# Latent attention's scores: three products of 96 rows become two passes of 128 rows and one of 32 rows on row groups

## The chip, the cores and the metric

One core of a Trainium2 chip runs the whole kernel. The metric is device time in microseconds (us): the time of one execution, median over the runs. Profiled executions come with a trace, whose span (from the first to the last instruction) is a little shorter than the execution's own time. PE is the matmul engine, PEld its loads of stationary operands, DVE the vector engine, ACT the scalar engine, POOL the third elementwise engine, and SP the queue that issues all DMAs of this kernel.

## The reference

One layer of an encoder trunk for 1024 tokens of 1024 channels in float32: a root-mean-square norm, one large input projection, then two attention mixers side by side (latent attention with 8 heads, and a dilated mixture), gated, projected, summed, projected again and added to the input. The change concerns the scores of latent attention. Cut to that:

```python
def mla_attention(c_q, c_kv, k_rope, positions, q_norm_g, kv_norm_g, w_uq, w_ukv):
    q = (rmsnorm(c_q, q_norm_g) @ w_uq).reshape(B, S, MLA_HEADS, MLA_QK_DIM)
    q = jnp.concatenate([q[..., :MLA_NOPE_DIM], rope(q[..., MLA_NOPE_DIM:], positions)], axis=-1)
    q = q * (MLA_QK_DIM ** -0.5)
    kv = (rmsnorm(c_kv, kv_norm_g) @ w_ukv).reshape(B, S, MLA_HEADS, MLA_NOPE_DIM + MLA_V_DIM)
    k_nope, v = kv[..., :MLA_NOPE_DIM], kv[..., MLA_NOPE_DIM:]
    k_pe = rope(k_rope[:, :, None, :], positions)
    k = jnp.concatenate([k_nope, jnp.broadcast_to(k_pe, (B, S, MLA_HEADS, MLA_ROPE_DIM))], axis=-1)
    ...
        s = jnp.einsum('bqhd,bkhd->bhqk', q_blk, k).astype(jnp.float32)
        p = jax.nn.softmax(s, axis=-1).astype(v.dtype)
        return jnp.einsum('bhqk,bkhd->bqhd', p, v)
```

A head's query and key have 96 channels: 64 of its own (`MLA_NOPE_DIM`) and 32 rotary ones (`MLA_ROPE_DIM`). The rotary part of the key is the same for all 8 heads.

## The kernel before

Every matmul of float32 values is done with operands in a rounded format (float32r in the code). A value is split into a high part, its rounding, and a low part, the rest. A product is then the sum of three matmuls, high by high, high by low and low by high, which `mm3` (lines 142 to 146) issues into one accumulator. In the profile these are the lines L144, L145 and L146, whatever the product is.

The kernel runs in stages. The first half (to about 530 us) does the projections. Inside it `latents` (line 338) makes the queries and keys of latent attention, half of the tokens at a time: `scaled` (line 390) scales a query tile of 128 channels by 512 tokens, splits it into the two halves of `mla_st` and stores them to HBM, the 64 own channels of each head to `s_qn`, the rotary ones to `s_qr`; the keys go to `s_kn` and the shared rotary key to `s_kp`. `mla_st` is a ring of two buffers. In this part a scheduler sets the order of instructions.

From about 538 us on the order is written out by hand. The dilated heads come first (to about 832 us), then latent attention (832 to about 1122 us), then the output projections. Latent attention is cut into 32 units; a unit is one head and 256 queries, that is two blocks b of 128 queries. `units` lists them: head by head, four units each, for heads 0 to 5; heads 6 and 7 alternate by two. `mla_tick(k, c)` (line 952) issues unit k in four steps c. Each step transposes a quarter of the unit's probabilities (`mla_transposes`, L852, four transposes into an accumulator called `bank`), splits them into a high part on ACT (L854) and a low part on DVE (L860), and multiplies an earlier quarter by the values (`mla_values`, L876 and L877). Step 0 also computes the scores of block 0 of the next unit, step 1 those of block 1; in steps 2 and 3 PE is given matmuls of other work (`feed`: the gates, then output projections). So in PE's queue the scores of unit k+1 stand among the transposes and value matmuls of unit k.

`mla_scores(k, b)` (line 814) is where the change is. A block's scores are 128 queries by 1024 keys and fill one of two accumulators, named `right` (block 0) and `left` (block 1) in the profile. For each half of the keys, 512 columns, it calls `mm3` with the 96 channels as rows: six matmuls per block, 12 per unit. Then DVE finds the maxima (L836) and ACT the exponentials (L844).

`mla_load_qk(h)` (line 799) loads a head's query and key from HBM to two buffers of 96 partitions that hold both parts, in five DMAs; it is called two heads ahead. `mla_load_v(h)` (line 809) loads its values into the ring `op_c`, of which it fills the first half of a place. All DMAs stand in one queue, SP, in the order of the code; one that must wait holds up those behind it. Buffers of the hand-ordered part appear as `at_r` and `at_f` in the profile.

At the end of the dilated part a last `combine` of dilated heads is spread over the first units of latent attention; it reads rows of factors from HBM (`s_rr`, twelve DMAs) and DVE multiplies by them (L1421).

Of the kernel before, what the change touches and what calls it, by code (L numbers as in the profile page):

```python
# [11 lines left out]
F32R = mybir.dt.float32r  # L12
# [7 lines left out]
S = 1024  # L20
# [40 lines left out]
class Net:  # L61
# [276 lines left out]
    def latents(self, up, lp, tp, pj):  # L338
# [4 lines left out]
        for half in range(2):  # L343
            c512 = slice(half * 512, half * 512 + 512)

            r = self.rcol[:, 4 * half:4 * half + 4]
# [7 lines left out]
            for t in range(4):  # L354
                c = self.lat[:, 4 * half + t]
# [15 lines left out]
            k = pt  # L371
# [18 lines left out]
            def scaled(src, dst):  # L390
                st = tp.tile([128, 2, 512], F32R, name="mla_st")
                nc.scalar.mul(st[:, 0], src, QK_SCALE)
                v.scalar_tensor_tensor(out=st[:, 1], in0=src, scalar=QK_SCALE, in1=st[:, 0].bitcast(F32), op0=ALU.mult, op1=ALU.subtract)
                self.dma(dst[:, :, c512], st)

# [3 lines left out]
            scaled(o1, self.qr[0])  # L399
            scaled(o2, self.qr[1])  # L400
            for j in range(4):
                scaled(up_q(slice(128 * j, 128 * j + 128)), self.qn[128 * j:128 * j + 128])
# [396 lines left out]
    def mla_load_qk(self, h):  # L799

        q, k = self.get("op_a", [96, 2, S], F32R), self.get("op_b", [96, 2, S], F32R)
        self.dma(q[0:64], self.qn[64 * h:64 * h + 64])
        for c in range(2):
            self.dma(q[64 + 16 * c:80 + 16 * c], self.qr[c][16 * h:16 * h + 16])
        self.dma(k[0:64], self.kn[64 * h:64 * h + 64])
        self.dma(k[64:96], self.kp)
        self.heads[h] = [q, k, None]

    def mla_load_v(self, h):

        vv = self.heads[h][2] = self.get("op_c", [128, 8, 128], F32R)
        self.dma(vv, self.mv.rearrange("(c p) x -> p c x", p=128)[:, :, 128 * h:128 * h + 128])

    def mla_scores(self, k, b):
# [7 lines left out]
        q, kk, _ = self.heads[h]  # L822
        qb = 2 * u + b
        qs = slice(128 * qb, 128 * qb + 128)
        s = self.get("s_mla", [128, S])
        for kb in range(2):
            ks = slice(512 * kb, 512 * kb + 512)
            self.mm3(s[:, ks], q[:, 0, qs], q[:, 1, qs], kk[:, 0, ks], kk[:, 1, ks], True, True)
        self.s[k, b] = s
# [693 lines left out]
    def run(self):  # L1523
        tc, nc = self.tc, self.nc
        with ExitStack() as ctx:
            dp = ctx.enter_context(tc.tile_pool(name="dram", bufs=1, space=DRAM))
            dt = lambda name, shape, d=F32: dp.tile(list(shape), d, name=name)
            self.qn, self.kn = dt("s_qn", (512, 2, S), F32R), dt("s_kn", (512, 2, S), F32R)
            self.qr, self.kp = dt("s_qr", (2, 128, 2, S), F32R), dt("s_kp", (32, 2, S), F32R)
# [163 lines left out]
```

## Time and profile before

| | us |
|---|---|
| median of 3 runs (lowest, highest) | 1263.55 (1259.07, 1266.88) |
| the profiled execution's own time | 1265.36 |
| its span | 1263.5 |
| PE busy, share of the span | 1214.5, 96% |
| DVE, ACT, POOL busy | 764.2, 621.0, 535.5 |
| mean granted PE clock | 0.992 |

Busy times are sums over the span; stages differ, so a share says little about one stage. A line of a timeline gives the start, the duration, the engine, the line of the kernel, the operation, what it writes and reads with partitions and elements, and, in brackets, the idle time of its engine just ahead and what ended it. Durations of matmuls overlap on PE: what one costs in a dense stream is the distance to the start of the next.

### The profile page before, as it was taken

What the parts mean: (1) busy time and instruction counts of PE and PEld (TensorE: products, weight loads), DVE (VectorE), ACT (ScalarE), POOL (GpSimd) and SP (SyncE); (2) the same over time, 40 slices, a digit from 0 to 9 for tenths busy, and PEclk for the clock granted to TensorE, in tenths of its full rate; (3) what the DMA queues carried; (4) which work ended last, traced back from release to release, by engine and by line L of the source; (5) the groups of instructions that cost most, each with busy time, mean ns of one, the idle gap of its engine ahead of it and who ended that gap; (6) DMA issues with size and microseconds to landing.
All of it is one profiled execution on the core that took longest, in us unless ns stands there. A gap on an engine that the chain in (4) does not pass through costs nothing.

```text
span 1263.5 us, 19551 instructions
## 1 busy us (share of the span) xinstructions
PE 1214.5 (96%) x6909; PEld 1063.2 (84%) x6909; DVE 764.2 (60%) x1373; ACT 621.0 (49%) x1300; POOL 535.5 (42%) x433
## 2 busy tenths in 40 slices
PE   8989999999999999999989899999899999989997
PEld 7979999788888888888878787978788888878886
DVE  7483524567567652345575776748777767659442
ACT  6533437344434345456554555636665655654232
POOL 2352217887777777445363230411420111157222
PEclk9989999999999999999999999999999999999999
DMA  9947675266556643497878797856543254234241
GB/s 325 274 152 264 224 283 159 84 177 167 138 135 158 169 125 117 129 260 205 207 207 211 186 259 191 240 156 165 154 140 105 81 126 125 93 101 167 84 150 50
DMA packets 131602, 212.99 MB, mean 169 GB/s; under 512 B 36841, under 2 KB 67121, under 8 KB 127601
## 3 DMA queue, kind: packets, MB, share of 16 engines
q1 hardware_dynamic: 131504, 211.75, 58.1%
q8 instruction: 54, 0.88, 0.3%
q14 instruction: 44, 0.35, 0.1%
HBM read 145.05 MB, written 66.65 MB: 168 GB/s over the span
## 4 chain that ended last, share of the span: by engine, by line
PE 72%; DMA 9%; DVE 8%; ACT 4%; issue 3%; POOL 2%; SPq 1%; ACTq 0%; DVEq 0%; POOLq 0%
PE bank L144 6%; PE bank L146 5%; PE bank L145 5%; PE bank L852 3%; PE st_a L144 2%; PE st_a L145 2%; PE st_a L146 2%; PE st_d L145 2%; PE st_c L145 2%; PE st_c L146 2%; PE st_d L146 2%; PE st_d L144 2%; PE st_c L144 2%; PE pj L144 2%; PE pj L145 2%
## 5 line engine op out<-in xcount | busy, mean ns | idle before, releaser
L151 POOL TENSOR_TENSOR w_l<-w_raw,w_h 128x512 fp32r<-128x512 f32 x188 | 246.7, 1326 | 300.1 <-ACT w_h L150 252.5
L150 ACT CAST w_h<-w_raw 128x512 fp32r<-128x512 f32 x188 | 112.4, 620 | 103.7 <-POOL w_raw L495 95.1
L144 PE MATMUL bank<-at_r,w_h 128*128 128x512 f32 x344 | 141.9, 412 | 5.6 <-DVE at_f L792 3.0
L860 DVE TENSOR_TENSOR at_r<-bank,at_r 128x512 fp32r<-128x512 f32 x128 | 87.9, 688 | 79.8 <-ACT at_r L854 79.5
L146 PE MATMUL bank<-at_r,w_l 128*128 128x512 f32 x344 | 135.3, 393 | 0.0
L145 PE MATMUL bank<-at_r,w_h 128*128 128x512 f32 x344 | 135.1, 393 | 0.0
L854 ACT CAST at_r<-bank 128x512 fp32r<-128x512 f32 x128 | 74.9, 585 | 81.0 <-PE bank L852 80.1
L144 PE MATMUL pj<-w_h,at_r 128*128 128x256 f32 x384 | 109.7, 286 | 0.0
L145 PE MATMUL pj<-w_l,at_r 128*128 128x256 f32 x384 | 109.4, 285 | 0.0
L146 PE MATMUL pj<-w_h,at_r 128*128 128x256 f32 x384 | 109.4, 285 | 0.0
L1116 ACT ACTIVATE at_f<-at_f,at_f 128x256 f32<-128x256 f32 x128 | 64.1, 501 | 70.8 <-DVE at_f L1109 70.7
L495 POOL TENSOR_TENSOR w_raw<-w_raw 128x512 f32<-128x512 f32 x64 | 83.7, 1308 | 0.0
L1135 DVE TENSOR_TENSOR at_r<-bank,at_r 128x512 fp32r<-128x512 f32 x64 | 44.0, 687 | 63.7 <-ACT at_r L1131 63.4
L852 PE MATMUL bank<-consts,at_f 128*128 128x128 f32 x512 | 77.0, 272 | 3.1 <-DVE at_r L860 2.0
L144 PEld LDWEIGHTS bank<-at_r,w_h 128*128 128x128 f32 x344 | 65.2, 190 | 16.8 <-DVE at_f L792 4.2
L146 PEld LDWEIGHTS bank<-at_r,w_l 128*128 128x128 f32 x344 | 64.8, 188 | 14.6
L144 PEld LDWEIGHTS pj<-w_h,at_r 128*128 128x128 f32 x384 | 74.2, 193 | 0.9
L145 PEld LDWEIGHTS pj<-w_l,at_r 128*128 128x128 f32 x384 | 74.1, 193 | 0.8
L146 PEld LDWEIGHTS pj<-w_h,at_r 128*128 128x128 f32 x384 | 74.1, 193 | 0.7
L145 PEld LDWEIGHTS bank<-at_r,w_h 128*128 128x128 f32 x344 | 65.3, 190 | 8.7
L876 PE MATMUL bank<-at_r,at_r 128*128 128x256 f32 x256 | 67.6, 285 | 1.9 <-ACT at_r L854 1.8
L877 PE MATMUL bank<-at_r,at_r 128*128 128x256 f32 x256 | 67.4, 285 | 1.8 <-DVE at_r L860 1.8
(320 smaller groups left out, 3331.1 us busy)
## 6 DMA issues: line engine op xcount, KB each, us to landing
w_raw<-wt SPq DMA_DIRECT2D x48, 512.0 KB, 4.4
at_r<-s_dq SPq DMA_DIRECT2D x32, 512.0 KB, 7.0
s_dq<-dq_st SPq DMA_DIRECT2D x80, 128.0 KB, 2.4
s_dk<-dq_st SPq DMA_DIRECT2D x80, 128.0 KB, 2.4
s_dv<-dv_st SPq DMA_DIRECT2D x32, 256.0 KB, 3.0
zt<-s_gt SPq DMA_DIRECT2D x32, 256.0 KB, 3.5
w_raw<-wv SPq DMA_DIRECT2D x12, 512.0 KB, 4.8
at_f<-s_rr SPq DMA_DIRECT2D x48, 128.0 KB, 3.2
```

The costliest lines, as they stand in the source:

```text
L144: mm(out, lh, rh, start=start, stop=False, skip_group_check=skip)
L145: mm(out, lh, rl, start=False, stop=False, skip_group_check=skip)
L146: return mm(out, ll, rh, start=False, stop=stop, skip_group_check=skip)
L150: self.nc.scalar.copy(out=h, in_=raw)
L151: sub.tensor_tensor(out=l, in0=raw, in1=h.bitcast(F32), op=ALU.subtract)
L495: self.nc.gpsimd.tensor_tensor(out=b[out], in0=b[x], in1=b[y], op=ALU.subtract)
L852: self.nc.tensor.transpose(pt[:, o:o + 128], self.P[k, b][:, 128 * kc:128 * kc + 128], self.ident)
L854: self.nc.scalar.copy(out=h, in_=pt)
L860: self.nc.vector.tensor_tensor(out=l, in0=pt, in1=h.bitcast(F32), op=ALU.subtract)
L876: mm(out, vv[:, kc], ph[:, x], start=kc == 0, stop=False)
L877: mm(out, vv[:, kc], pl[:, x], start=False, stop=kc == 7)
L1116: nc.scalar.activation(out=p, in_=p, func=AF.Exp, scale=-1.0, bias=nm, accum_out=den)
```

## The change

The 288 rows of a score product (96 for each of the three products) are laid out anew. A query buffer of 128 partitions and two halves holds in its first half the 96 high channels and again the high channels 0 to 31, in its second half the high channels 32 to 95 and the low channels 0 to 63. The key buffer holds the matching rows: high 0 to 95 with low 0 to 31, then low 32 to 95 with high 0 to 63. Two matmuls of 128 rows thus cover 256 of the 288 rows. The remaining 32 are the low rotary channels of the query by the high rotary channels of the key. They are computed ahead of the others by matmuls on 32 partitions each: the four of a unit (two blocks by two halves of the keys) read four different groups of 32 partitions and are placed on four row groups of the array (`tile_position`), each writing its own 512 columns of an accumulator. The full matmuls then add to them.

For this, `scaled` stores high and low parts of all query channels apart, in a tensor `s_qd` (head, part, 96 channels, tokens), with two DMAs for each tile. `mla_load_qk` issues ten DMAs. A new function `mla_load_rest` loads the query's 32 rows, spread over the four groups, with four more into the second half of a place of `op_c`; it is called just ahead of the load of the values, for head 0 at the end of `mla_load_qk`, where the shared rotary key is also loaded, once, into four groups with four DMAs.

```diff
-            def scaled(src, dst):
+            def scaled(src, heads, rows):
                 st = tp.tile([128, 2, 512], F32R, name="mla_st")
                 nc.scalar.mul(st[:, 0], src, QK_SCALE)
                 v.scalar_tensor_tensor(out=st[:, 1], in0=src, scalar=QK_SCALE, in1=st[:, 0].bitcast(F32), op0=ALU.mult, op1=ALU.subtract)
-                self.dma(dst[:, :, c512], st)
-
+                for p in range(2):
+                    self.dma(self.qd[heads, p, rows, c512], st[:, p])
...
-        q, k = self.get("op_a", [96, 2, S], F32R), self.get("op_b", [96, 2, S], F32R)
-        self.dma(q[0:64], self.qn[64 * h:64 * h + 64])
-        for c in range(2):
-            self.dma(q[64 + 16 * c:80 + 16 * c], self.qr[c][16 * h:16 * h + 16])
-        self.dma(k[0:64], self.kn[64 * h:64 * h + 64])
-        self.dma(k[64:96], self.kp)
-        self.heads[h] = [q, k, None]
+        q, k = self.get("op_a", [128, 2, S], F32R), self.get("op_b", [128, 2, S], F32R)
+        qd, kn = self.qd[h], self.kn[64 * h:64 * h + 64]
+        self.dma(k[0:64, 0], kn[:, 0])
+        self.dma(k[64:96, 0], self.kp[:, 0])
+        self.dma(q[0:96, 0], qd[0])
+        self.dma(q[96:128, 0], qd[0, 0:32])
+        self.dma(k[96:128, 0], kn[0:32, 1])
+        self.dma(q[0:64, 1], qd[0, 32:96])
+        self.dma(q[64:128, 1], qd[1, 0:64])
+        self.dma(k[0:32, 1], kn[32:64, 1])
+        self.dma(k[32:64, 1], self.kp[:, 1])
+        self.dma(k[64:128, 1], kn[:, 0])
+        self.heads[h] = [q, k, None, None]
+        if h == 0:
+            self.mla_load_rest(h)
+
+    def mla_load_rest(self, h):
+
+        place = self.places["op_c"][self.turn["op_c"] % 2]
+        x = self.heads[h][3] = self.shaped(place + 4096, [128, 512], F32R)
+        for r in range(4):
+            src = self.qd[h, 1, 64:96].rearrange("r (u b t) -> b r u t", b=2, t=128)[r // 2]
+            self.dma(x[32 * r:32 * r + 32].rearrange("r (u t) -> r u t", t=128), src)
+        if h == 0:
+            self.kr = self.shaped(place + 6144, [128, 512], F32R)
+            for r in range(4):
+                self.dma(self.kr[32 * r:32 * r + 32], self.kp[:, 0, 512 * (r % 2):512 * (r % 2) + 512])
 
     def mla_load_v(self, h):
 
+        if h:
+            self.mla_load_rest(h)
         vv = self.heads[h][2] = self.get("op_c", [128, 8, 128], F32R)
...
-        q, kk, _ = self.heads[h]
+        mm = self.nc.tensor.matmul
+        q, kk, _, rest = self.heads[h]
+        for y in ((b,) if k == 0 else (0, 1) if b == 0 else ()):
+            s = self.s[k, y] = self.get("s_mla", [128, S])
+            for kb in range(2):
+                r = slice(64 * y + 32 * kb, 64 * y + 32 * kb + 32)
+                mm(s[:, 512 * kb:512 * kb + 512], rest[r, 128 * u:128 * u + 128], self.kr[r], start=True, stop=False, skip_group_check=True, tile_position=(r.start, 0))
         qb = 2 * u + b
         qs = slice(128 * qb, 128 * qb + 128)
-        s = self.get("s_mla", [128, S])
+        s = self.s[k, b]
         for kb in range(2):
             ks = slice(512 * kb, 512 * kb + 512)
-            self.mm3(s[:, ks], q[:, 0, qs], q[:, 1, qs], kk[:, 0, ks], kk[:, 1, ks], True, True)
-        self.s[k, b] = s
+            for c in range(2):
+                mm(s[:, ks], q[:, c, qs], kk[:, c, ks], start=False, stop=c == 1, skip_group_check=True)
```

How PE's queue reads around the scores of block 0 of a unit, before: four transposes of step 0, the six matmuls of the block into `right`, the value matmuls (L876, L877), the transposes of step 1, behind which the six of `left` stand in the same way.

```order
L852 MATMUL bank_5420<-consts,at_1024_f 128x128 x4
L144 MATMUL right_8235<-at_2048_r 128x512
L145 MATMUL right_8235<-at_2048_r 128x512
L146 MATMUL right_8235<-at_2048_r 128x512
L144 MATMUL right_8235<-at_2048_r 128x512
L145 MATMUL right_8235<-at_2048_r 128x512
L146 MATMUL right_8235<-at_2048_r 128x512
L876 MATMUL bank_5422<-at_512_r,at_1024_r 128x256
L877 MATMUL bank_5422<-at_512_r,at_1024_r 128x256
L876 MATMUL bank_5422<-at_512_r,at_1024_r 128x256
L877 MATMUL bank_5422<-at_512_r,at_1024_r 128x256
L852 MATMUL bank_5419<-consts,at_1024_f 128x128 x4
```

The same place of PE's queue after the change, where the transposes are L880, the values L904 and L905, the 32-row matmuls L850 and the full ones L857:

```order
L880 MATMUL bank_5431<-consts,at_1024_f 128x128 x4
L850 MATMUL right_8266<-at_512_r 128x512 x2
L850 MATMUL left_8300<-at_512_r 128x512 x2
L857 MATMUL right_8266<-at_2048_r 128x512 x4
L904 MATMUL bank_5433<-at_512_r,at_1024_r 128x256
L905 MATMUL bank_5433<-at_512_r,at_1024_r 128x256
L904 MATMUL bank_5433<-at_512_r,at_1024_r 128x256
L905 MATMUL bank_5433<-at_512_r,at_1024_r 128x256
L880 MATMUL bank_5430<-consts,at_1024_f 128x128 x4
L857 MATMUL left_8300<-at_2048_r 128x512 x4
```

The four 32-row matmuls of both blocks stand together in step 0, and each block has four full matmuls, so that step 1 holds four where it held six.

SP's queue at the load of head 2, before, between the store of the combination's factors and their twelve loads:

```order
L140 DMA s_rr<-at_512_f 16x6x64
L140 DMA at_2048_r<-s_qn 64x2048
L140 DMA at_2048_r<-s_qr 16x2048 x2
L140 DMA at_2048_r<-s_kn 64x2048
L140 DMA at_2048_r<-s_kp 32x2048
L140 DMA at_512_f<-s_rr 64x512 x12
```

And after:

```order
L140 DMA s_rr<-at_512_f 16x6x64
L140 DMA at_2048_r<-s_kn 64x1024
L140 DMA at_2048_r<-s_kp 32x1024
L140 DMA at_2048_r<-s_qd 96x1024
L140 DMA at_2048_r<-s_qd 32x1024
L140 DMA at_2048_r<-s_kn 32x1024
L140 DMA at_2048_r<-s_qd 64x1024 x2
L140 DMA at_2048_r<-s_kn 32x1024
L140 DMA at_2048_r<-s_kp 32x1024
L140 DMA at_2048_r<-s_kn 64x1024
L140 DMA at_512_f<-s_rr 64x512 x12
```

The twelve loads stand behind ten DMAs instead of five.

More of the change, by code (lines that the diff above doesn't have):

```diff
@@ L393, in scaled @@
                 v.scalar_tensor_tensor(out=st[:, 1], in0=src, scalar=QK_SCALE, in1=st[:, 0].bitcast(F32), op0=ALU.mult, op1=ALU.subtract)
-                self.dma(dst[:, :, c512], st)
+                for p in range(2):
+                    self.dma(self.qd[heads, p, rows, c512], st[:, p])
             pa, pb = up_q(slice(512, 640)), up_q(slice(640, 768))
             o1, o2 = self.rope(pa, pb, cos, sin, tp)
-            scaled(o1, self.qr[0])
-            scaled(o2, self.qr[1])
+            scaled(o1, slice(0, 8), slice(64, 80))
+            scaled(o2, slice(0, 8), slice(80, 96))
             for j in range(4):
-                scaled(up_q(slice(128 * j, 128 * j + 128)), self.qn[128 * j:128 * j + 128])
+                scaled(up_q(slice(128 * j, 128 * j + 128)), slice(2 * j, 2 * j + 2), slice(0, 64))
             for j in range(4):
@@ L1527, in run @@
             dt = lambda name, shape, d=F32: dp.tile(list(shape), d, name=name)
-            self.qn, self.kn = dt("s_qn", (512, 2, S), F32R), dt("s_kn", (512, 2, S), F32R)
-            self.qr, self.kp = dt("s_qr", (2, 128, 2, S), F32R), dt("s_kp", (32, 2, S), F32R)
+            self.qd, self.kn = dt("s_qd", (8, 2, 96, S), F32R), dt("s_kn", (512, 2, S), F32R)
+            self.kp = dt("s_kp", (32, 2, S), F32R)
             self.mv = dt("s_mv", (S, 1024), F32R)
```

## The prediction

> **What bounds the kernel now.** I read the page's chain first, then busy time by stage, then who makes PE wait, and last the single instructions of one score product. The page's chain, and the stretches of latent attention (length, then busy us of PE, of its weight loads, of DVE, ACT and POOL, then the granted clock and the DMA share):
>
> ```profile
> PE 72%; DMA 9%; DVE 8%; ACT 4%; issue 3%; POOL 2%; SPq 1%; ACTq 0%; DVEq 0%; POOLq 0%
> ```
> ```profile
> 842.00:900.00 58.00, 55.95 (x338) 48.94 (x337) 47.06 (x72) 34.72 (x63) 17.27 (x13) 1.00 0.51 141
> 960.00:1020.00 60.00, 59.19 (x366) 52.36 (x365) 42.33 (x55) 34.19 (x63) 7.66 (x6) 1.00 0.43 104
> ```
>
> The reader is to see that PE is busy for 56 of 58 and 59 of 60 us at full clock, while DVE and ACT are a fifth to two fifths idle. The stage is bound by PE, and time taken off PE's stream there is time off the end, as long as nothing else becomes late. What a matmul costs is the distance between starts, not its duration, because the records overlap. One product of 128 queries by 1024 keys, between four transposes and the value matmuls, in the timeline of PE:
>
> ```profile
> 867.60 0.60 PE L852 MATMUL bank<-consts,at_f 128*128 128x128 f32 x4
> 867.96 0.47 PE L144 MATMUL right<-at_r 96*128 96x512 f32 x1
> 868.27 0.39 PE L145 MATMUL right<-at_r 96*128 96x512 f32 x1
> 868.49 0.39 PE L146 MATMUL right<-at_r 96*128 96x512 f32 x1
> 868.72 0.40 PE L144 MATMUL right<-at_r 96*128 96x512 f32 x1
> 868.96 0.39 PE L145 MATMUL right<-at_r 96*128 96x512 f32 x1
> 869.19 0.40 PE L146 MATMUL right<-at_r 96*128 96x512 f32 x1
> 869.42 0.28 PE L876 MATMUL bank<-at_r,at_r 128*128 128x256 f32 x1
> 869.54 0.29 PE L877 MATMUL bank<-at_r,at_r 128*128 128x256 f32 x1
> ```
>
> Six matmuls take 869.42 - 867.96 = 1.46 us: five steps of 0.23 and a first one of 0.31. The 0.39 us that each is recorded for holds 0.16 us in which the next already streams. A matmul of 256 columns steps by 0.12.
>
> **The change, term by term.**
>
> *Full matmuls.* A unit (one head, 256 queries) has two products, so 12 matmuls; the change leaves 8 of them and adds one pack of four of 32 rows. The first step after the transposes keeps its 0.08 in both. With P for what a pack occupies of PE's stream, a unit saves 4 x 0.23 - P = 0.92 - P. A row of 128 partitions instead of 96 costs nothing that I can see: the matmuls of both heights are paced by 512 columns, and their weight loads last as long (the groups by line; behind the bar busy us, mean ns, idle us):
>
> ```profile
> L145 PEld LDWEIGHTS right<-at_r 96*128 96x128 f32 x64 | 12.1, 190 | 1.4
> L145 PEld LDWEIGHTS right<-at_r 128*128 128x128 f32 x32 | 6.0, 189 | 1.0
> ```
>
> *The pack, P.* No matmul of this trace stands on one row group, so P is bounded. Upper end: the four take turns, P = 4 x 0.23 = 0.92, no gain. Lower end: all four stream together, P = 0.23. Between them lies the weight load: each of the four brings its own 128 columns. The nearest row is the class matmuls of 64 columns, where little streams and each has its own load:
>
> ```profile
> 743.47 1.87 PEld L1211 LDWEIGHTS right<-at_f,at_f 128*128 128x128 f32 x16
> 745.25 0.19 PEld L144 LDWEIGHTS bank<-at_r,w_h 128*128 128x128 f32 x1
> ```
>
> Sixteen loads, from 743.47 to the next one at 745.25, are 1.78 / 16 = 0.11 us each. (Their operands are plain floats, so the row doesn't say whether load or stream sets that step; it is what one load and a short matmul cost here.) I take it that streams overlap and loads come one behind another: three steps of 0.11 and the last stream of 0.23, P = 0.33 + 0.23 = 0.56. A unit then saves 0.92 - 0.56 = 0.36. There are 32 units; the very first runs its two pairs apart, each at 0.11 + 0.23 = 0.34, and saves 0.92 - 0.68 = 0.24. Sum: 31 x 0.36 + 0.24 = **-11.4 us**. Ends: 31 x 0.69 + 0.46 = -21.9 at P = 0.23, and 0 at 0.92.
>
> *The second accumulator.* The pack writes the rows of both query blocks a third of a unit earlier than the second block's scores ran, so it needs the accumulator `left` earlier. Its last reader is the exponential of the unit before:
>
> ```profile
> 957.74 1.12 ACT L844 ACTIVATE at_f<-left,m_nm 128x1024 f32<-128x1024 f32 x1
> 958.75 0.20 ACT L844 ACTIVATION_READ_ACCUMULATOR at_f<-left,m_nm 128x1 f32 x1
> ...
> 961.17 0.60 PE L852 MATMUL bank<-consts,at_f 128*128 128x128 f32 x4
> ```
>
> It ends at 958.95, and the transposes that read its result go ahead of the pack on PE anyway, at 961.17. Cost 0; the cover is 2.2 us.
>
> *Loads of a head.* Before, five DMAs of 1.5 MB; now ten of 2.0 MB, and later four small ones for the 32 rows. Most heads are loaded four units (some 36 us) ahead and the queue waits for PE there, so they cost nothing. At two places the queue is full. One is head 2, in whose wake twelve loads of the last combination stand:
>
> ```profile
> 863.32 0.45 SPq L140 DMA_DIRECT2D at_r<-s_qn  x1
> 863.82 2.12 SPq L140 DMA_DIRECT2D at_r<-s_qr  x2
> 865.98 0.45 SPq L140 DMA_DIRECT2D at_r<-s_kn  x1
> 866.48 0.58 SPq L140 DMA_DIRECT2D at_r<-s_kp  x1
> 867.15 9.91 SPq L140 DMA_DIRECT2D at_f<-s_rr  x12
> ```
> ```profile
> q1 hardware_dynamic: 1122, 2.98, 82.8%
> ```
> ```profile
> 871.94 1.22 DVE L836 TENSOR_REDUCE m_nm<-left 128x1 f32<-128x1024 f32 x1
> 875.12 0.69 DVE L1421 TENSOR_TENSOR at_f<-at_f,at_f 128x512 f32<-128x512 f32 x1 [1.96 <-DMA at_f<-s_rr]
> ```
> ```profile
> 877.44 0.39 PE L877 MATMUL bank<-at_r,at_r 128*128 128x256 f32 x1 [0.84 <-DVE at_r L860]
> ```
>
> DVE stands 1.96 us for those rows at 875.12; behind it in its queue is the low half of a probability tile, and PE stands 0.84 us for that. Any further delay goes through one to one. By bytes it is 0.5 MB more at 0.21 MB per us (the row of the queues, taken from 862 to 878, has 2.98 MB, and its first 2 us are empty), 2.4 us; by count it is five issues at 9.91 / 12 = 0.83, 4.1 us. Between the two: **+3 us** (0 to 5).
>
> The other place is head 0, loaded at the end of the dilated part:
>
> ```profile
> 809.83 0.68 SPq L140 DMA_DIRECT2D at_r<-s_qn  x1
> 810.56 1.04 SPq L140 DMA_DIRECT2D at_r<-s_qr  x2
> 811.64 0.47 SPq L140 DMA_DIRECT2D at_r<-s_kn  x1
> 812.15 0.58 SPq L140 DMA_DIRECT2D at_r<-s_kp  x1
> 812.78 0.52 SPq L140 DMA_DIRECT2D w_raw<-wt  x1
> ```
> ```profile
> 832.92 0.48 PE L144 MATMUL right<-at_r 96*128 96x512 f32 x1
> ```
>
> Five issues become 18, among them the shared rotary key, which the very first pack needs. At 0.83 each they take 15 us instead of 3, to about 825, and must have landed by 832.9: covered by some 3 us when a landing takes 5. Head 1's ten, the stores of gates and the values of head 0 move back by up to 10 us behind them, and a gate's buffer may come free late. I take **+1 us** (0 to 5). For head 7 the four small loads come one unit ahead instead of four; a unit is 9 us, so they are covered, with the least room of the heads.
>
> *Stores of the queries.* Twelve stores of 512 KB become 24 of half the size; the first half leaves one DVE operation earlier, the second one issue later. The two buffers behind them hold ACT up, not PE:
>
> ```profile
> ACT mla_st L392 <- DMA s_qn<-mla_st: 7.4, 4, 3.9
> ```
> ```profile
> PE pj L144 <- DVE mla_st L151: 0.4, 1, 0.4
> ```
>
> PE waited 0.4 us in this whole part, since projections of values fill it. The block sums come after it, though, and PE stands 2.76 us before the first block product, so a shift of the part can show there: **0** (-2 to +2).
>
> **The sum.** -11.4 + 3 + 1 + 0 = -7.4 us. The profiled execution took 1265.36 us (1263.5 of span and 1.9 around it), so 1258.0 for it; it ran 1.8 above the median of 1263.55, and against the median I say **1256 us**.
>
> **Rivals.**
>
> *All four at once.* If loads into different row groups overlap too, P = 0.23, the gain is 21.9, and 1263.55 - 21.9 + 4 = 1245.7 us. For it: loads of 0.19 us stand beside running matmuls throughout the trace. Against it: nothing here shows two loads under way less than 0.1 us apart. The Trainium skill, page "TensorE: Matmul & The Clock Gate", section "Part 3: Packing small matmuls — row/col tiling", reports 3.07 times the rate for four row tiles of 32 rows and 512 columns. By that, as an estimate, P would be 0.92 / 3.07 = 0.30 us and the time near 1248 us; no run here shows it yet.
>
> *Switching empties the array.* If PE must let the last wave out before it changes between full height and row groups, each change costs the hidden 0.39 - 0.23 = 0.16 us. There are 33 packs and two changes for each: 66 x 0.16 = 10.6 us, and 1256.1 + 10.6 = 1266.7 us. For it: the whole of the gain hangs on overlap between neighbours. Against it: the change from transposes to matmuls, the only one of kind in this trace, costs 0.08 us. The Trainium skill, page "TensorEngine Tiling (Array Packing)", section "Key Properties", says that changing the tiling mode, not merely the tile, drains the engine. By that rule this rival would hold; no row of before has such a change.
>
> *Turns only.* The four stream one after another, P = 0.92: only the loads' price is left, 1267.5 us.
>
> *Slower.* Turns and emptying together: P = 0.92 + 0.32 = 1.24 us, 32 units lose about 0.32, 1267.5 + 10.6 = 1278 us. It decides from the point where a pack with its changes costs more than 0.92 + (12.6 - 4) / 32 = 1.19 us, 12.6 being 1% of the time. For it speaks that both halves are unknown; against it, that row groups are separate partitions of both operands and separate banks of the result, so nothing I see makes them take turns.
>
> **How the numbers follow.** About 1% is what a measurement of this kernel can tell from no change. Forecast 0.34, all at once 0.26, emptying 0.20, turns only 0.09, slower 0.11. Faster by over 1% (below 1250.9): most of all-at-once, 0.22, and the forecast's low edge, 0.03, make 0.25. Slower by over 1% (above 1276.2): 0.08 of the slower case and 0.04 for heads that come late, 0.12. The rest, 0.63, lies within 1%. The range goes from 1243 (all at once with a cheap queue) to 1271 (turns with a dear queue).
>
> **What would show it.** In the timeline of one unit, the distance from the start of the first 32-row matmul to the first full one is P with its changes: 0.56 for the forecast, 0.23 to 0.3 for all at once, 0.7 to 0.9 with emptying, 0.92 or more for turns. The full matmuls should step by 0.23 as before, the stage be some 11 us shorter, and DVE's wait for the combination's rows grow from 1.96 to about 5 us. I would be wrong if PE stood for the 32-row loads of a head, or if the change of heights cost more than its hidden tail.

## The result and the profile after

| | before | after |
|---|---|---|
| median of the runs, us | 1264.84 (1259.07 to 1266.88) | 1354.97 (1353.23 to 1357.57) |
| profiled execution, span, us | 1263.5 | 1351.5 |
| start to first block product | 226.0 | 295.2 |
| from there to the first row maximum of latent attention | 608.6 | 626.8 |
| from there to the last row maximum of `right` (the stage) | 280.8 | 281.4 |
| from there to the end | 148.1 | 148.0 |

The changed kernel is slower by a ratio of 1.072 (95%: 1.068 to 1.076), 88.0 us of span. The last four rows are taken from the starts of the same instructions in both traces, and their differences add up to it: +69.3, +18.2, +0.6, -0.1. Nearly the whole loss lies ahead of the stage that was changed, and that stage itself has gained nothing. Two runs further down, one of the kernel with both edits (1689.89 us) and one of the kernel before (1350.29 us), were in a slow state with a lower granted clock (0.752 and 0.849); they enter no ratio, and the trace of the first is not used.

The page's chain after, by engine and by line:

```profile
PE 61%; DMA 14%; DVE 8%; ACT 3%; issue 3%; SPq 2%; POOL 1%; ACTq 0%; DVEq 0%
DMA s_qd<-mla_st 6%; PE bank L144 5%; PE bank L146 5%; PE bank L145 5%; PE bank L880 3%; PE right L857 2%; SPq L140 2%; PE st_a L144 2%; PE st_a L146 2%; PE st_d L146 2%; PE st_c L146 2%; PE st_a L145 2%; PE st_d L145 2%; PE st_c L145 2%; PE st_c L144 2%
```

PE carried 72% of the chain before. Now a transfer leads the list of lines: the stores of the scaled queries.

**The part that stores the queries.** Two stretches of it, before and then after (length, busy us of PE, its weight loads, DVE, ACT and POOL, granted clock, DMA share, GB/s):

```profile
85.00:182.00 97.00, 96.63 (x695) 91.26 (x693) 47.10 (x75) 37.66 (x71) 24.74 (x18) 1.00 0.68 250
182.00:226.00 44.00, 41.24 (x345) 41.03 (x343) 17.39 (x13) 25.80 (x47) 30.03 (x20) 1.00 0.52 171
```
```profile
85.00:182.00 97.00, 68.92 (x419) 63.35 (x418) 30.48 (x50) 23.41 (x43) 18.55 (x13) 0.81 0.40 142
182.00:226.00 44.00, 22.70 (x122) 20.04 (x121) 6.19 (x11) 4.71 (x9) 0.01 (x1) 0.80 0.26 91
```

PE was full here and now stands three tenths to a half of the time, and the granted clock is 0.81 and 0.80. The transfers are not busier but idler: 142 and 91 GB/s where 250 and 171 were moved. Two steps of the chain in that part (start, length, what), who waits for these tiles (us, times and, where a third number stands, the longest), and the DMA engines from 90 to 240 us in 40 slices (tenths busy, GB/s):

```profile
107.57 18.57 DMA s_qd<-mla_st
...
128.96 18.33 DMA s_qd<-mla_st
```
```profile
ACT mla_st L392 <- DMA s_qd<-mla_st: 56.5, 8, 10.4
```
```profile
  PE pj L144: 55.9, 12
```
```profile
DMA  2363211112111771964852158551131112116118
GB/s 81 90 188 87 110 51 51 51 51 112 51 51 51 256 274 56 352 250 185 350 210 76 72 151 240 160 190 45 51 113 51 50 51 113 51 51 235 51 45 333
```

A store of 256 KB from two heads holds the chain for 18.3 to 18.6 us in these steps. Where these stores are alone, the 16 DMA engines are 10 to 19% busy and move 51 GB/s, slice after slice, as much as two of sixteen at work. The tile of a store is not free until it has landed, ScalarE waits for the tile, VectorE's low half comes behind ScalarE's high half, and the projections (`pj`) wait until VectorE has read their bank: 55.9 us in 12 waits of PE, where it was 0.4 in one.

**The end of the dilated part.** The first matmul after a gap, and the matmuls that follow it:

```profile
892.10 1.19 PE L1182 MATMUL left<-at_r,at_r 128*128 128x256 f32 x4 [13.85 <-DMA at_r<-s_kp]
...
898.21 0.63 PE L146 MATMUL bank<-at_r,w_l 128*128 128x512 f32 x1
898.63 0.63 PE L144 MATMUL bank<-at_r,w_h 128*128 128x512 f32 x1
```

PE stands 13.85 us before the last dilated item's values, released by a transfer of the rotary keys, and then steps by 0.43 us instead of 0.23 until about 901.

**The changed stage.** One unit in a clean place, steps 0 and 1:

```profile
1050.74 0.60 PE L880 MATMUL bank<-consts,at_f 128*128 128x128 f32 x4
1051.27 0.50 PE L850 MATMUL right<-at_r 32*128 32x512 f32 x2
1051.28 0.50 PE L850 MATMUL left<-at_r 32*128 32x512 f32 x2
1051.71 1.19 PE L857 MATMUL right<-at_r 128*128 128x512 f32 x4
1052.74 0.28 PE L904 MATMUL bank<-at_r,at_r 128*128 128x256 f32 x1
...
1053.31 0.60 PE L880 MATMUL bank<-consts,at_f 128*128 128x128 f32 x4
1053.66 1.19 PE L857 MATMUL left<-at_r 128*128 128x512 f32 x4
1054.69 0.27 PE L904 MATMUL bank<-at_r,at_r 128*128 128x256 f32 x1
```

The two pairs of 32-row matmuls start within 0.01 us of one another and last 0.50 us each: they run side by side, which two experiments below test. From the transposes to the values step 0 takes 2.00 us (1.82 before, by the prediction's rows) and step 1 takes 1.38 (by the same view of before, 869.91 to 871.74, it took 1.83). This unit saves 0.27 us, and 32 such units would save 8.6. But only every second unit runs like this. In the others step 1 takes 1.59 to 1.98 us, as here, where it takes 1.72:

```profile
1061.56 0.60 PE L880 MATMUL bank<-consts,at_f 128*128 128x128 f32 x4
1061.92 1.18 PE L857 MATMUL left<-at_r 128*128 128x512 f32 x4
1063.28 0.39 PE L904 MATMUL bank<-at_r,at_r 128*128 128x256 f32 x1 [0.18 <-DVE at_f L920]
```

The stage as a whole shows no gain, and the waits say where to look: the rows of the combination's factors, and weight loads of PE.

```profile
963.77 0.69 DVE L1449 TENSOR_TENSOR at_f<-at_f,at_f 128x512 f32<-128x512 f32 x1 [3.45 <-DMA at_f<-s_rr]
```
```profile
966.03 0.55 PE L905 MATMUL bank<-at_r,at_r 128*128 128x256 f32 x1 [2.54 <-DVE at_r L888]
```
```profile
PEld bank L904 <- DVE at_f L920: 8.5, 14, 0.9
PEld right L857 <- issue: 7.6, 30, 0.4
PEld right L850 <- issue: 5.0, 29, 0.3
```

In the kernel before, the wait like the first of these three rows read:

```profile
PEld bank L876 <- DVE at_f L892: 1.5, 6, 0.6
```

### The profile page after: what moved, and what is told of

Read it like the earlier page. It is cut to its first block, busy times and chain, and to the rows that moved or that the text cites. A ratio compares the mean times of both kernels' runs of the same rounds, so it can differ in the third digit from the quotient of the medians.

```text
span 1351.5 us, 19658 instructions
## 1 busy us (share of the span) xinstructions
PE 1233.8 (91%) x6909; PEld 1065.4 (79%) x6909; DVE 760.9 (56%) x1373; ACT 622.6 (46%) x1300; POOL 536.6 (40%) x433
## 4 chain that ended last, share of the span: by engine, by line
PE 61%; DMA 14%; DVE 8%; ACT 3%; issue 3%; SPq 2%; POOL 1%; ACTq 0%; DVEq 0%
DMA s_qd<-mla_st 6%; PE bank L144 5%; PE bank L146 5%; PE bank L145 5%; PE bank L880 3%; PE right L857 2%; SPq L140 2%; PE st_a L144 2%; PE st_a L146 2%; PE st_d L146 2%; PE st_c L146 2%; PE st_a L145 2%; PE st_d L145 2%; PE st_c L145 2%; PE st_c L144 2%
## 5 line engine op out<-in xcount | busy, mean ns | idle before, releaser
L144 PE MATMUL bank<-at_r,w_h 128*128 128x512 f32 x344 | 143.4, 417 | 5.8 <-DVE at_f L792 3.0
L145 PE MATMUL bank<-at_r,w_h 128*128 128x512 f32 x344 | 136.7, 397 | 0.0
L146 PE MATMUL pj<-w_h,at_r 128*128 128x256 f32 x384 | 114.4, 298 | 0.0
L145 PE MATMUL pj<-w_l,at_r 128*128 128x256 f32 x384 | 114.3, 298 | 0.0
L144 PE MATMUL pj<-w_h,at_r 128*128 128x256 f32 x384 | 114.3, 298 | 0.0
L145 PEld LDWEIGHTS pj<-w_l,at_r 128*128 128x128 f32 x384 | 79.6, 207 | 1.5
L880 PE MATMUL bank<-consts,at_f 128*128 128x128 f32 x512 | 77.5, 273 | 3.1 <-DVE at_r L888 2.0
L144 PEld LDWEIGHTS pj<-w_h,at_r 128*128 128x128 f32 x384 | 79.4, 207 | 1.0
L146 PEld LDWEIGHTS pj<-w_h,at_r 128*128 128x128 f32 x384 | 79.3, 207 | 0.9
L904 PE MATMUL bank<-at_r,at_r 128*128 128x256 f32 x256 | 68.4, 289 | 3.9 <-DVE at_f L920 2.0
L905 PE MATMUL bank<-at_r,at_r 128*128 128x256 f32 x256 | 67.2, 284 | 4.0 <-DVE at_r L888 4.0
```

The lines of the kernel that those rows point to most:

```text
L144: mm(out, lh, rh, start=start, stop=False, skip_group_check=skip)
L145: mm(out, lh, rl, start=False, stop=False, skip_group_check=skip)
L146: return mm(out, ll, rh, start=False, stop=stop, skip_group_check=skip)
L880: self.nc.tensor.transpose(pt[:, o:o + 128], self.P[k, b][:, 128 * kc:128 * kc + 128], self.ident)
L904: mm(out, vv[:, kc], ph[:, x], start=kc == 0, stop=False)
L905: mm(out, vv[:, kc], pl[:, x], start=False, stop=kc == 7)
```

## The experiments

Each kernel is the changed one with the edit that its diff shows. "The stage" is the stretch of the table above. Runs of one group share their runs of the kernel before. A stretch is read from one trace of each kernel, and equal code does not take equal time in every trace: in the eight packed kernels from the rotary rows on, which share the part ahead of the first block product, that product starts between 220.1 and 224.7 us.

**The stores alone.** A store of the plain rows of two heads (2 x 64 x 512) goes to a layout where it is 128 x 512; the count and the bytes of the stores stay. The load of a head then takes 12 transfers instead of 10.

```diff
-                    self.dma(self.qd[heads, p, rows, c512], st[:, p])
+                    self.dma(dst(p), st[:, p])
...
-                scaled(up_q(slice(128 * j, 128 * j + 128)), slice(2 * j, 2 * j + 2), slice(0, 64))
+                scaled(up_q(slice(128 * j, 128 * j + 128)), lambda p: self.qn[p, 128 * j:128 * j + 128, c512])
```

> The changed kernel with the same 24 stores of the queries and the same bytes, but the 64 rows of 'no position' of two heads go to a layout whose outermost run is 128 rows instead of 2 heads; the load of a head takes 12 transfers instead of 10. Theory A (a transfer is spread over the 16 DMA engines by its outermost dimension, so a store of 2x64x512 runs on 2 of them, 18.3 to 18.6 us instead of 3 to 6, and these stores hold up the tiles of the queries and the array): the first product of the block returns from 295.2 to about 226 us and the time falls by some 69 us to about 1285. Rival B (the 69 us come from the number or the small packets of the stores, not from their shape): the stores still land late and the time stays within 20 us of 1355. The stop of 13.9 us before the last dilated values (892 us in the changed kernel) should stay in both.

Measured: 1289.0 us in one run, first block product at 230.9 us. The stop at the dilated values stayed. The page of DMA issues in that part:

```profile
s_qn<-mla_st SPq DMA_DIRECT2D x16, 256.0 KB, 2.0
```

Theory A: the same bytes in as many transfers land in 2.0 us, and 64.3 of the 69.3 us are gone. The Trainium skill, page "DMA: Bandwidth & Descriptors", section "Why a DMA increments its semaphore by 16 and not by 1", says that the number of engines is the largest one up to 16 that divides the slowest dimension of both access patterns; two heads give 2. The 51 GB/s and the digit 1 (10 to 19% of sixteen) agree with it.

**The value tile alone.**

```diff
-            o["v"] = self.get("op_c", [128, 9, 128], F32R)
+            o["v"] = self.get("op_c", [128, nch, 128], F32R)
```

> The changed kernel with one size changed: the value tile of a dilated item holds as many chunks of keys as the item has, not 9, so the last item's tile no longer covers the rows that the first head's 32-row strips are loaded into. Theory A (the stop of 13.9 us at the last dilated values is a wait for those loads through the overlap of the two tiles): the stop goes, and with the half clock behind it some 14 to 18 us, to about 1337 to 1341. Rival B (the array stops there because its instructions arrive late behind the 18 transfers of the head's load): the stop stays and the time is 1355 +- 3.

Measured: 1340.29 us in one run. The only wait of PE from 840 to 908 us:

```profile
PE bank L1151 <- ACT at_f L1144: 3.4, 5, 1.4
```

Theory A: the stop of 13.85 us is gone, and the stretch to the first row maximum takes 611.1 us instead of 626.8, 15.7 less. The tile was declared with nine chunks and used with eight; the first head's strips lie in the ninth, so the values waited for transfers that wrote where they never read. With the stop gone another, shorter one comes up at the start of the stage: PE stands 2.83 us before the first scores of `left`, behind a wait of VectorE of 6.46 us for a store of the gates. In the changed kernel PE stood 0.80 us there, as before the change (0.83), and VectorE did not wait for that store.

**Both.** The two edits above.

> Both edits together: stores over 128 outer rows, and the value tile no longer over the strips. If both theories A hold, the two losses add: 1355 - 69 - 14 to 18 = 1268 to 1272, which is then what the packing itself does, against 1264.8 before. With the stores alone right: about 1285. With neither: 1355.

Measured: 1268.38 us, ratio to before 1.0029 (1.0006 to 1.0051). The two losses add as expected, and what is left is within about 0.5% of the kernel before.

**Without the pass of 32 rows** (on both edits).

```diff
-                mm(s[:, 512 * kb:512 * kb + 512], rest[r, 128 * u:128 * u + 128], self.kr[r], start=True, ...)
+                pass
...
-                mm(s[:, ks], q[:, c, qs], kk[:, c, ks], start=False, stop=c == 1, skip_group_check=True)
+                mm(s[:, ks], q[:, c, qs], kk[:, c, ks], start=c == 0, stop=c == 1, skip_group_check=True)
```

> Both edits, and the pass of 32 rows is left out: no product of the low rotary rows of the queries with the high rows of the keys, so the scores lack one of four parts of the rotary term. It prices the pass with its two changes of tile size. Theory A (four 32-row matmuls run side by side and the array empties at both changes, 0.65 us a unit read from unit starts): 32 units by 0.65 = 21 us less than the run with both edits, about 1248. Rival B (the pass is hidden beside a wait of each unit): within 5 us of the run with both edits. Rival C (the passes run one after the other, 1.2 us): 38 us less.

Measured: 1261.23 us in one run, 7.2 below the median with both edits, so neither the 21 of theory A nor the 5 of rival B; the stage 268.6 us, 12.2 less than the 280.8 of the run with the stores alone, the nearest trace. One step 0:

```profile
873.80 0.60 PE L882 MATMUL bank<-consts,at_f 128*128 128x128 f32 x4
874.16 1.17 PE L859 MATMUL right<-at_r 128*128 128x512 f32 x4
875.18 0.27 PE L906 MATMUL bank<-at_r,at_r 128*128 128x256 f32 x1
```

In the unit the pass costs 2.00 - 1.38 = 0.62 us, as A has it, 19.8 us for 32. The stage gave back only 12.2 of them: freed of the pass, PE waits 7.5 us in 14 waits for the sum of values on VectorE, against 2.0 in 8 with it, and in every second unit step 1 takes 2.05 us in the mean instead of 1.70. So the stage is near a second bound. PE also stands 4.2 us at the first scores of `left`, where it stood 0.8 in the run with the stores alone; that is the store of the gates again, which the stop at the dilated values hid there, and no effect of the pass.

**The rotary rows as well.** The halves of a head's rotary rows are interleaved in memory (those of the shared key likewise), so that their eight stores (8 x 16 x 512) also become 128 x 512.

```diff
-            scaled(o1, lambda p: self.qp[:, p, 0:16, c512])
+            scaled(o1, lambda p: self.qp[p, 0:256:2, c512])
...
```

> The kernel with both edits, and the rotary rows of the queries kept with the two halves of a head's rows interleaved, so that their 8 stores too run over 128 outer rows (they ran over 8), at the same number of transfers everywhere. With the stores of 8x16x512 left, the first product of the block still started at 229.9 to 230.9 us against 226.0 before, and ScalarE waited 16 us for these stores. Theory A (same mechanism as for the 2x64 stores): the start returns to 226 to 227 us and the time falls by 3 to 5 us from 1268.4 to 1264 to 1265. Rival B (the lost 4 to 5 us come from 24 stores instead of 12): the start stays at 230 and the time at 1268.

Measured: 1265.95 us, ratio 1.0024 (1.0009 to 1.0039); the first block product at 220.1 us. For the start that is theory A, with ScalarE's wait for these stores halved from 15.8 us (stores alone) to 7.8. For the time it is not shown: the ratio went from 1.0029 to 1.0024, and the two intervals overlap. This trace, too, has a stand at the first scores of `left`, 3.5 us, that comes up again below.

**All four on one row group** (on the run with the rotary rows).

```diff
-                r = slice(64 * y + 32 * kb, 64 * y + 32 * kb + 32)
+                r = slice(0, 32)
```

> The run with the interleaved rotary rows, but all four matmuls of 32 rows take the rows of row group 0, so that they must run one after the other; the strips of the other groups are loaded and not used, so the scores get the wrong low rotary part in three of four quarters. If the four ran side by side before, each unit gains three matmuls of 512 columns at 0.22 to 0.23 us: 0.67 by 32 = +21 us on the stage of latent attention (280.8 us from the first to the last row maximum of the right accumulator). If they took turns anyway: no change, within 3 us.

Measured: 1282.09 us in one run, the stage 299.7 us against 282.5, so +17.2. One unit:

```profile
868.47 0.60 PE L882 MATMUL bank<-consts,at_f 128*128 128x128 f32 x4
869.00 0.73 PE L852 MATMUL right<-at_r 32*128 32x512 f32 x2
869.57 0.62 PE L852 MATMUL left<-at_r 32*128 32x512 f32 x2
870.13 1.19 PE L859 MATMUL right<-at_r 128*128 128x512 f32 x4
871.16 0.28 PE L906 MATMUL bank<-at_r,at_r 128*128 128x256 f32 x1
```

Step 0 takes 2.69 us, 0.69 more than side by side, three matmuls of 0.23. So the row groups do work at once, loads and streams. Of 22 us for 32 units the stage shows 17; that the rest went into waits which the longer units cover is likely, but was not traced.

**The pass issued twice** (on the same run).

```diff
+        for again in range(2):
+            for y in ys:
+                for kb in range(2):
...
```

> The run with the interleaved rotary rows, but the pass of 32 rows is issued twice in each unit, the second writing the same values over the first. It splits the pass's price of 0.65 us a unit into the pass itself and the emptying of the array at the two changes of tile size. If the pass itself is 0.23 us and the rest is emptying: the stage grows by 32 by 0.23 = 7 us. If the pass itself takes 0.5 to 0.65 and emptying nothing: by 16 to 21 us.

Measured: 1273.27 us in one run, the stage 285.6 us, +3.1. One unit:

```profile
871.43 0.60 PE L885 MATMUL bank<-consts,at_f 128*128 128x128 f32 x4
871.96 0.50 PE L855 MATMUL right<-at_r 32*128 32x512 f32 x2
...
872.30 0.40 PE L855 MATMUL right<-at_r 32*128 32x512 f32 x2
...
872.63 1.19 PE L862 MATMUL right<-at_r 128*128 128x512 f32 x4
873.66 0.28 PE L909 MATMUL bank<-at_r,at_r 128*128 128x256 f32 x1
```

Step 0 takes 2.23 us, so a second pass adds 0.23. The pass itself is 0.23 us, and of its price of 0.62 the other 0.39 is left for the two changes of height. The weight loads point there too: in the changed kernel those of the 32-row matmuls wait 5.0 us in 29 waits and those of the full ones behind them 7.6 in 30, 0.17 and 0.25 us each, for nothing that the profile shows. The stage grew by less than half of 32 x 0.23: by the unit the split is clear, by the stage it is not.

**The load of the next head one step later** (on the run with the rotary rows).

```diff
             self.mla_weighted(k - 1)
-            h, u = self.units[k + 1] if k + 1 < 32 else (7, 3)
-            if u == 3 and h < 6:
-                self.mla_load_qk(h + 2)
...
             if c == 2:
                 self.mla_merged(k - 1, self.nc.gpsimd)
+                h, u = self.units[k + 1] if k + 1 < 32 else (7, 3)
+                if u == 3 and h < 6:
+                    self.mla_load_qk(h + 2)
```

> The run with the interleaved rotary rows, and the load of the head after the next issued one step later, so that the 12 rows of factors (s_rr) of the last dilated pair are queued ahead of its 12 transfers. In the changed kernel VectorE waited 3.5 us for these rows (2.9 with the stores mended, 2.0 before the change), TensorE 2.5 us behind it, and then ran at a lower clock for some 3 us. Theory A (this wait takes back part of the gain): the wait falls to about 0 and the stage of latent attention from 280.8 to 276 to 278 us. Rival B (the wait is covered by the next unit): within 1 us.

Measured: 1262.56 us, ratio 0.999 (0.9974 to 1.0005); the stage 278.6 us, 3.9 less. VectorE's wait for the rows of factors (2.9 us in two waits) is gone, and the clock granted from 870 to 890 us is 1.00 instead of 0.91. Theory A. In this trace one stand is left at the start of the stage, seen on VectorE and on PE:

```profile
833.94 0.69 DVE L718 TENSOR_TENSOR zt<-bank,at_f 128x512 f32<-128x512 f32 x1 [6.64 <-DMA s_gt<-zt]
```
```profile
836.79 0.89 PE L852 MATMUL left<-at_r 32*128 32x512 f32 x2 [3.00 <-issue]
...
839.91 0.63 PE L145 MATMUL bank<-at_r,w_h 128*128 128x512 f32 x1
```

VectorE waits for a buffer of the gates whose store stands on SP behind the second head's load. The row maxima, the copy that frees `left` and PE stand behind it.

**The second head's load later too.**

```diff
-        for h in range(2):
-            items.append((lambda h=h: self.mla_load_qk(h), lambda h=h: self.mla_load_v(h)))
+        items.append((lambda: self.mla_load_qk(0), lambda: self.mla_load_v(0)))
+        items.append((lambda: None, lambda: None))
...
+            if k == 0 and c == 2:
+                self.mla_load_qk(1)
+            if k == 0 and c == 3:
+                self.mla_load_v(1)
```

> The run with the late load of the next head, and the second head's load too is issued later, in the third and fourth step of the first unit instead of at the end of the dilated part. There the 12 transfers and 4 strips stand on the one queue ahead of a store of the gates; VectorE waits 6.6 us for that store with the row maxima behind it, TensorE stands 3.0 us before the first scores of the left accumulator and then runs at 0.43 us a matmul instead of 0.23 for some 7 us. Theory A (the longer load costs this): the wait goes and the time falls by 4 to 6 us, from 1262.6 to 1257 to 1259. Rival B (the accumulator's own release is as late): within 1 us.

Measured: 1258.07 us against 1264.14 before, ratio 0.9959 (0.9942 to 0.9975). The stand falls from 3.00 to 0.79 us, the stretch to the first row maximum from 611.4 to 606.8, the stage to 277.2. Theory A. This is the fastest kernel of the study, and it beats the one before by 0.4%.

**The same two moves in the unpacked kernel.** The edit is that of the last two diffs, on the kernel before.

> The kernel before the change, unpacked, with the two later loads alone (the head after the next one step later, the second head in the first unit). It tells how much of the last version's gain is the packing's. In the kernel before, VectorE waited 2.0 us for the rows of factors and TensorE 0.8 us before the first left scores, so I expect 0 to -2 us, 1261.5 to 1263.5; if the moves are worth as much there as in the packed kernel (-8 us), the packing gains nothing.

Measured: 1264.05 us, ratio 1.000 (0.9977 to 1.0024), the stage 279.8 us. The moves alone are worth nothing there; they only take back what the longer loads of the packed layout had cost. The worth of the packed kernel, once its transfers are out of the way, is the difference of the last two: 1264.05 - 1258.07 = 6.0 us. By their traces only 2.6 of it lies in the stage, where the packing acts. The rest lies in other parts; one piece of it is that the first block products of the unpacked trace run 7 steps at half speed, some 1.4 us, and those of the packed one none.

**The sum ahead of the row maxima** (on the run with the next head's load later), and the same with the second head's load later too:

```diff
-            self.mla_maxima(k + 1, 0)
             self.mla_sum(k - 1)
+            self.mla_maxima(k + 1, 0)
```

> The run with the late load of the next head, and in each unit's first step VectorE adds the finished values (the sum that frees the bank of the values) ahead of the row maxima instead of behind them. With the pass packed the first two steps of a unit are shorter and TensorE waits for this sum: 2.0 us in 8 waits (weight loads 8.9 us in 15), against 0.2 (1.5 in 6) before the change. Theory A (this wait takes back some of the gain): the wait falls below 0.5 us and the stage from 278.5 to 275 to 277 us. Rival B (the maxima come later by the sum, and the exponentials behind them hold up the next transposes): the stage stays or grows.

> All mended: stores over 128 rows, value tile off the strips, both later loads and the sum ahead of the maxima. If the late loads and the sum are each worth what theory A says of them: 1255 to 1258, below the kernel before (1263.5) by 0.4 to 0.7%, which is what the prediction gave to the packing alone. If the sum ahead costs (rival B): 1258 to 1262.

Measured: 1277.36 us in one run with the stage at 291.8; 1267.63 us, ratio 1.0031 (1.0016 to 1.0046), with the stage at 286.2. Rival B, and worse than it said. In the first of the two traces PE no longer waits for the sum, but ScalarE's exponentials wait 26.0 us in 19 waits for the row maxima (8.6 in 7 without the edit). PE's own loss shows in steps 2 and 3: it waits 6.4 us in 7 waits for VectorE's products of the output projections, 3.0 in 5 without the edit, and after the longest of these waits, 1.86 us, it steps by 0.43 us.

**The bank of the values freed by ScalarE** (on the fastest kernel, and on the unpacked one with the same moves).

```diff
             self.nc.scalar.copy(out=t, in_=self.av[64:128])
+            self.nc.scalar.copy(out=self.nums[h // 2, u // 2][x], in_=self.av[0:64])
...
-            self.nc.vector.tensor_tensor(out=n, in0=self.av[0:64], in1=self.av_t, op=ALU.add)
+            self.nc.vector.tensor_tensor(out=n, in0=n, in1=self.av_t, op=ALU.add)
```

> The run with both later loads, and ScalarE copies both halves of the finished values out of their bank (0.58 us each), so that VectorE adds them from SBUF and the bank is free without the row maximum of 1.2 us ahead of that sum. Theory A (this bank's release takes back the packing's gain in every second unit): the second step of these units falls from 2.16 to 2.52 us towards 1.83, TensorE's wait for the sum (2.0 us in 8) goes to 0, and the stage falls from 277.2 by 3 to 6 us, to 271 to 274; the time from 1258 to 1252 to 1255. Rival B (ScalarE's extra copy delays the next casts and exponentials as much as it saves): the stage within 1 us of 277 or longer.

> The unpacked kernel before with the two later loads and the same two copies on ScalarE. There the wait for the sum was 0.2 us in one wait, so nothing is to be gained: the stage stays at 279 to 281 us and the time at 1262 to 1266. The packing's own worth is then this run less e12: by theory A some 8 to 11 us, by rival B 6 as between the runs without the copies.

Measured: 1263.38 us, ratio 0.9993 (0.9973 to 1.0014), the stage 279.2; unpacked 1266.56 us, ratio 1.0025 (1.0008 to 1.0041), the stage 283.0 in a trace of its slowest run. The weight loads of PE, before the edit and with it:

```profile
PEld bank L906 <- DVE at_f L922: 8.5, 14, 0.9
```
```profile
PEld bank L144 <- DVE at_f L792: 6.5, 7, 1.8
...
PEld bank L906 <- ACT at_f L918: 4.7, 14, 0.3
```

The wait for this bank fell from 8.5 to 4.7 us, but the output projections that share the stage now wait 6.5 us for their VectorE products where it was 4.2, and both kernels' stages grew, by 2.0 and 3.2 us. Rival B for the stage and the time. Yet theory A's mechanism is in the trace: in every second unit step 1 falls from a median of 1.71 us to 1.43, so it was this bank that held PE there. That returns some 4 us, and steps 2 and 3 of the units lose 4.8. That freeing the bank in another way would return the gain was not shown, and a second bank for the values was not tried. Between these two kernels the packed one is worth 1266.56 - 1263.38 = 3.2 us, less than the 6.0 above.

## Why the prediction was wrong, point by point

- **"Stores of the queries ... 0 (-2 to +2)" is the step that failed.** It counted bytes and issues and did not look at the form: `s_qd` is written as 2 x 64 x 512 and 8 x 16 x 512, where `s_qn` was written as 128 x 2 x 512. Measured +69.3 us; 64.3 of them went with the rows made outermost at the same count and bytes.
- **"The other place is head 0 ... I take +1 us (0 to 5)"** failed as well. The text counted the wait of the first pack for its rows (which never came) and not who else lay in the way. Measured +18.2 us, which is the stop of 13.85 us and the half speed behind it. It came from the overlap of the strips with the ninth chunk of a value tile, and 15.7 us went with that chunk. The other 2.5 came back as another stand, behind the second head's load, where a store of the gates stood. The sentence that a gate's buffer "may come free late" named that second mechanism. It cost nothing in the changed kernel, where the stop hid it; with the next head's load moved it was a stand of 3.00 us and some 6 us at half speed, and moving the second head's load took 4.6 us off the stretch (611.4 to 606.8).
- **"The stage is bound by PE, and time taken off PE's stream there is time off the end, as long as nothing else becomes late"** held only with its condition. Something else became late: the bank of the values. In every second unit a new sum starts in it, and with step 1 down from 1.83 to 1.38 us the values would reach it before VectorE has freed it behind a row maximum. 8.5 us of weight loads stand there, against 1.5 before. Set side by side step for step, the 30 units from the second to the last but one should save 8.1 us; step 1 and the values behind it lose some 5.6 of them in every second unit, and the combination's rows take 3.2 at one place. No term of the sum looked at the bank.
- **The full matmuls** were right: 0.45 us less in step 1 where nothing holds it up, two of 0.23.
- **The pack, "P = 0.56"**: with its changes 0.62 us. The size was near, the make-up wrong. Loads of different row groups do not come one behind another; all four start at once and the pass takes 0.23, the rival "all four at once". And the two changes of height cost 0.39 us together, as in the rival "switching empties the array", which had 0.32; that it is an emptying is an inference from the price and from the waits of the weight loads. Both were right in their prices, and that their sum is close to the forecast's is luck. The sign that was named for it, the distance from the first 32-row matmul to the first full one, reads 0.44 us and holds only the pass and the second change; the other 0.17 lies ahead of the first 32-row matmul, 0.53 us behind the transposes where it was 0.36. Two rivals that exclude each other in their prices need not exclude each other in the machine.
- **The Trainium skill**, page "TensorE: Matmul & The Clock Gate", section "Part 3: Packing small matmuls — row/col tiling", gave P = 0.30 us, as an estimate, by its 3.07 times; the added pass measures 0.23 here. The Trainium skill's page "TensorEngine Tiling (Array Packing)", section "Key Properties", agrees with what is left for two changes, 0.39 us.
- **Head 2's load, "+3 us (0 to 5)"** was right in size: step for step, 3.2 us. The wait behind it was not: VectorE's went from 1.96 to 3.45 us, not to about 5, and PE's from 0.84 to 2.54; the rest of the 3.2 us is PE at half speed behind its wait, of which the forecast said nothing. Moving the load out of the way brought 3.9 us in the stage of the packed kernel, and both moves together 1.0 in that of the unpacked one.
- **The second accumulator, 0**, was right: in the changed kernel PE waits for `left` once, 0.80 us in the first unit, as before (0.83). In the kernels without the stop it is late there, through the store of the gates.
- **The forecast of the whole**: with the stores and the tile mended the time is 1268.38 us, and with the loads moved as well 1258.07. The 1256 us forecast needed a kernel whose transfers cost nothing, and those were the terms taken as small. That 1258.07 comes close to it does not confirm the sum: its stage is 3.6 us shorter than in the kernel before (277.2 against 280.8), where the sum had 8.4 with head 2's load, and the rest of the gain lies outside.

## What to carry to other kernels

When a change lays a tensor out anew in memory, read every store and load of it as an access pattern on both sides: what stands outermost decides how many DMA engines work on it, and here the same bytes in as many transfers took 2.0 us or 18.3 to 18.6. When a load is given a new place in SBUF, look at what the tiles there are declared to cover, not at what they use. And before counting what a bound engine saves, find the next buffer that it would reach too early.

## What the runs showed of the hardware

- The speed of a transfer follows its form: stores with 2 heads outermost moved 51 GB/s and took 18.3 to 18.6 us, and the same bytes as 128 rows landed in 2.0 us.
- Four matmuls of 32 rows on four row groups cost as much of PE as one, 0.23 us; the two changes between that height and 128 cost 0.39.
- After some short stands PE steps at half speed. A stand of 3.00 us (the run with the next head's load later) was followed by matmuls stepping 0.43 us until about 843 us, some 6 us; one of 1.73 us (the run with the rotary rows) by four matmuls recorded over 2.07 us instead of 1.19. The Trainium skill, page "TensorE: Matmul & The Clock Gate", section "Part 1: The HAM clock gate (the "warmup" mystery)", puts it at one idle window of about 3.4 us; both stands here are shorter. The length of the stand does not decide it alone: in the kernel before, one of 2.98 us at 674 us was followed by matmuls stepping 0.23 us.
